# A triangular inverse's first level in a decoder layer: two split steps each become one run of small matmuls, and the first starts later

## The chip, the cores and the metric

The kernel runs on one core of one Trainium2 chip. The metric is device time in microseconds (us) for one execution. TensorE does the matmuls; VectorE (DVE in the profile), ScalarE (ACT) and GpSimd (POOL) move and combine their results; SyncE (SP) and GpSimd issue the DMAs. Matmul results land in PSUM, of which a tile here takes one bank of 128 x 512 float32.

## The reference: one hybrid decoder layer

For 256 tokens of width 1024 the layer computes, cut to what matters:

```python
h = rms_norm(x, norm1_g)
proj = h @ w_in                                  # 5408 columns: RWKV, attention, gates
y_a = rwkv7_time_mix(shift-mixed proj[:1824])    # 8 heads of 64, delta-rule state update per token
y_b = moba_attention(q, k, v)                    # 8 heads; 256 tokens are one block: causal softmax
x = x + (sigmoid(g_a) * (y_a @ w_branch_a) + sigmoid(g_b) * (y_b @ w_branch_b)) @ w_out
h2 = rms_norm(x, norm2_g)
x = x + (gelu(causal_conv3(h2 @ w_up_a)) * (h2 @ w_up_b)) @ w_down
```

and the RWKV recurrence, token by token, with a state of 64 x 64 for each head:

```python
sa = state @ a_t
state = state * w_t + outer(sa, b_t) + outer(v_t, k_t)
y_t = state @ r_t
```

## The kernel before

The recurrence is worked in four chunks of 64 tokens. Within a chunk each of the 8 heads needs the inverse of a unit lower triangular 64 x 64 matrix: 32 inverses (8 heads x 4 chunks), in tiles with an index `u` of 16 and a half `q` of 2. The inverse is built from its diagonal blocks. Blocks of 16 x 16 are inverted on VectorE (`Xb`) and carried by DMAs through DRAM into `X0` and `X`, which hold them where TensorE wants them (lines 757 to 778; DMAs alternate between the queues of GpSimd and SyncE). Then two levels of matmuls follow:

- first level, 16 to 32, for the two 32-halves `h` of each matrix. First step (line 851, tile `pp`): `G` times `X0`, 32 small products for each `h`, copied to `P` by ScalarE (line 857) and VectorE (858). Second step (865, `px`): `X` times `P` for `h = 0`, added into `X0` on VectorE. Third step (880, tile `pxt`): `P` times `X`, 32 small products for each `h`, copied into `X` by ScalarE (888);
- second level, 32 to 64: `pp` again with 32 columns (894), copies to `P`, `pxt` with 32 columns (905), copies into `X`.

A small product here has a 32-row, 16- or 32-column stationary part on a quarter of TensorE's rows; as float32 it is two matmul instructions.

After the inverse the recurrence over the four chunks `c` begins: `pz` (961), `Z0` (965), `pu` (970), `VU` (974, 975), `pS` (981), `Sn` (987 to 990), `pyt` (997, 1002). A third thread, `group_norm`, takes each chunk's output and turns it (`pc`, line 940). Attention turns q and k (`pqk`, 1080), makes scores (`ps`, 1101), a softmax on VectorE and ScalarE (1112 to 1119), turns the weights (`ppt`, 1129) and sums the values (`po`, 1141).

The large products are the weight matmuls. Float32 weights come in chunks of 128 x 1024 (`raw`), are split into a high part (`whi`, ScalarE, 263) and a low part (`wlo`, VectorE, 273), and each product is done three times (high-high, high-low, low-high). In `wst` (lines 301, 303, 306) a block of 12 products of 256 columns stands between two yields; in `xst` (322, 323, 326) a block of 6 products of 512 columns.

The order in which instructions are written is set by hand with generators: `chain` (all of the recurrence), `bulk` (the input projections, the gates, the first branch projection), and, begun by these, `attention` and `group_norm`. Each `yield cost, delay` says how long the piece just written keeps a model clock, and how long after that the thread may go on. The loop takes the first thread in the list that may go on:

```python
cost, lat = next(th[1])
now_t += cost
th[2] = now_t + lat
```

`chain` stands ahead of `bulk` in the list. So a `yield 0, 5.5` in `chain` lets `bulk` write large products for 5.5 units of that clock; a block costs 1.32 (`wst`) or 1.3 (`xst`). With `yield 0.6, 2.5` between two steps two blocks come between. The framework then schedules the instructions of each engine by this order as priority; `tc.high_priority()` moves the marked ones ahead. After the loop the second branch projection (`branch(0, ...)`), the output projection and the channel mixing follow, large products nearly throughout.

Of the kernel before, what the change touches and what calls it, by code (L numbers as in the profile page):

```python
# [36 lines left out]
def body(tc, x, positions, norm1_g, w_in, rwkv_mu, w_decay_up, decay_bias, w_aaa_up,  # L37
# [5 lines left out]
    with ctx:  # L43
# [22 lines left out]
        def b2(name, shape, dt=F32):  # L66
            return sb.tile(shape, dt, name=name, tag="b2", bufs=9)
# [495 lines left out]
        def chain():  # L563
# [275 lines left out]
            def quad(side, h):  # L839
                return slice(64 * side + 32 * h, 64 * side + 32 * h + 32)  # L840

            def two_banks(nm, n):
                return [chp(nm)[:, 0:8 * n].rearrange("p (u n) -> p u n", n=n) for _ in range(2)]

            yield 0, 5.5
            pp = two_banks("pp", 16)
            for h in range(2):
                for i in range(8):
                    for q, a in QA:
                        u = 8 * a + i  # L850
                        pe.matmul(pp[q][quad(1 - a, h), i], G[q][quad(1 - q, h), u, 32 * h:32 * h + 32],
                                  X0[quad(1 - q, h), u, 0:16], start=True, stop=True)
                if h == 0:
                    yield 0.6, 2.5
            P = b2("P", [128, 2, 8, 16])
            with tc.high_priority():
                act.copy(P[:, 0], pp[0])
# [18 lines left out]
            for h in range(2):  # L876
                for u in range(16):
                    for a in range(2):
                        s_ = quad(1 - a, h)
                        pe.matmul(pt[s_.start:s_.start + 16, u], P[s_, u // 8, u % 8],  # L880
                                  X[s_, u, 32 * h + 16:32 * h + 32], start=True, stop=True)
                if h == 0:
                    yield 0.6, 2.5
            for h in range(2):
                for a in range(2):
                    r0 = quad(a, h).start
# [339 lines left out]

        now_t = 0.0
        threads = [["chain", chain(), 0.0], ["bulk", bulk(), 0.0]]
        while threads:
            th = next((h for h in threads if h[2] <= now_t), None)  # L1230
# [191 lines left out]
```

## Time and profile before

| | us |
|---|---|
| median of 3 runs | 407.1 |
| lowest, highest | 406.77, 407.61 |
| the profiled execution, own time | 407.71 |
| its span | 405.6 |
| TensorE busy in the span | 399.1 |
| VectorE, ScalarE, GpSimd busy | 317.8, 234.3, 44.5 |
| first step (L851), first and last matmul start | 103.0, 107.2 |
| third step (L880), first and last matmul start | 114.3, 119.3 |

The profile is one execution; its rows name an engine, a line, an operation, and the tiles it writes and reads (`out<-in`). PE is TensorE's matmuls, PEld its loads of stationary operands. Consecutive matmuls overlap, so a row's busy time says less than the distance between two starts.

### The profile page before, as it was taken

How to read it: one execution, taken by the hardware profiler on the slowest of the kernel's cores; microseconds unless marked ns; L12 is line 12 of the kernel's file. 1: busy time of each engine (PE TensorE's matmuls, PEld its weight loads, DVE VectorE, ACT ScalarE, POOL GpSimd, SP SyncE). 2: the span in 40 equal slices, each digit the busy share in tenths (PEclk: the TensorE clock that was granted, in tenths of full speed). 3: DMA queues.
4: the chain of work that ended last, by engine and by line, in shares of the span. 5: the costliest groups of instructions: out<-in, count | busy, mean ns of one | idle time of the engine just before them, and what ended most of it. 6: DMA issues, size and time to landing. Idle time of an engine off the chain costs nothing.

```text
span 405.6 us, 8306 instructions
## 1 busy us (share of the span) xinstructions
PE 399.1 (98%) x3286; PEld 348.0 (86%) x3286; DVE 317.8 (78%) x539; ACT 234.3 (58%) x395; POOL 44.5 (11%) x72
## 2 busy tenths in 40 slices
PE   6999999999999999999999999999999999999996
PEld 3899899888899898999888888888888888888885
DVE  3888999869576797687965897967869778697694
ACT  5999665365464975453554764555545455365450
POOL 7810510122320010000000000000000000000000
PEclk9999999999999999999999999999999999999999
DMA  8983556755845244446665657566655656656612
GB/s 238 315 255 101 160 155 161 205 137 136 229 114 152 55 156 125 159 136 198 178 197 155 200 161 214 160 210 200 207 185 176 207 178 188 205 174 197 199 56 105
DMA packets 60193, 70.35 MB, mean 173 GB/s; under 512 B 7608, under 2 KB 50506, under 8 KB 60154
## 3 DMA queue, kind: packets, MB, share of 16 engines
q1 hardware_dynamic: 59222, 69.40, 57.2%
q0 software_dynamic: 880, 0.41, 0.6%
q8 instruction: 26, 0.43, 0.4%
q14 instruction: 13, 0.11, 0.1%
q10 hardware_dynamic: 52, 0.01, 0.0%
HBM read 68.37 MB, written 1.44 MB: 172 GB/s over the span
## 4 chain that ended last, share of the span: by engine, by line
PE 92%; DVE 3%; DMA 1%; ACT 1%; issue 1%; POOL 0%; SPq 0%; ACTq 0%
PE acc L1303 20%; PE acc L1308 10%; PE acc L301 8%; PE acc L306 7%; PE acc L303 7%; PE acc L322 5%; PE acc L326 5%; PE acc L323 5%; PE f L1325 4%; PE f L1323 4%; PE f L1327 4%; PE idle L466 1%; DMA x<-in_x_dram 1%; PE pgr L687 1%; DVE sc L1119 1%
## 5 line engine op out<-in xcount | busy, mean ns | idle before, releaser
L263 ACT CAST whi<-raw 128x1024 fp32r<-128x1024 f32 x122 | 127.8, 1052 | 110.8 <-PE acc L1303 42.5
L273 DVE TENSOR_TENSOR wlo<-raw,whi 128x1024 fp32r<-128x1024 f32 x122 | 149.5, 1228 | 38.6 <-PE acc L1308 14.0
L1303 PE MATMUL acc<-hx,whi 128*128 128x512 f32 x352 | 89.5, 396 | 0.0
L1303 PEld LDWEIGHTS acc<-hx,whi 128*128 128x128 f32 x352 | 63.5, 188 | 12.4
L301 PE MATMUL acc<-hx,whi 128*128 128x256 f32 x224 | 56.9, 289 | 0.0
L303 PE MATMUL acc<-hx,whi 128*128 128x256 f32 x224 | 54.6, 279 | 0.0
L1308 PEld LDWEIGHTS acc<-hx,wlo 128*128 128x128 f32 x352 | 46.8, 188 | 4.0
L1308 PE MATMUL acc<-hx,wlo 128*128 128x256 f32 x352 | 47.4, 277 | 0.0
L301 PEld LDWEIGHTS acc<-hx,whi 128*128 128x128 f32 x224 | 42.2, 189 | 2.5 <-issue 1.4
L303 PEld LDWEIGHTS acc<-hx,whi 128*128 128x128 f32 x224 | 42.2, 189 | 0.1
L306 PE MATMUL acc<-hx,wlo 128*128 128x256 f32 x224 | 35.0, 278 | 0.0
L1325 PE MATMUL f<-whi,hb 128*128 128x512 f32 x80 | 31.2, 390 | 0.0
L1323 PE MATMUL f<-whi,hb 128*128 128x512 f32 x80 | 31.2, 390 | 0.0
L1327 PE MATMUL f<-wlo,hb 128*128 128x512 f32 x80 | 31.2, 390 | 0.0
L306 PEld LDWEIGHTS acc<-hx,wlo 128*128 128x128 f32 x224 | 30.0, 189 | 0.0
L1313 DVE TENSOR_REDUCE an<-acc 128x256 f32<-128x512 f32 x22 | 14.2, 685 | 9.4 <-PE acc L1308 9.3
L322 PE MATMUL acc<-whi,hx 128*128 128x512 f32 x48 | 19.5, 406 | 0.0
L323 PE MATMUL acc<-whi,hx 128*128 128x512 f32 x48 | 18.8, 392 | 0.0
L1327 PEld LDWEIGHTS f<-wlo,hb 128*128 128x128 f32 x80 | 15.0, 188 | 3.2
L1323 PEld LDWEIGHTS f<-whi,hb 128*128 128x128 f32 x80 | 15.0, 188 | 2.8
L1325 PEld LDWEIGHTS f<-whi,hb 128*128 128x128 f32 x80 | 15.0, 188 | 2.7
L326 PE MATMUL acc<-wlo,hx 128*128 128x512 f32 x48 | 14.9, 393 | 0.0
(336 smaller groups left out, 627.8 us busy)
## 6 DMA issues: line engine op xcount, KB each, us to landing
raw<-in_w_ffn_up_dram SPq DMA_DIRECT2D x44, 512.0 KB, 4.2
raw<-in_w_in_dram SPq DMA_DIRECT2D x41, 512.0 KB, 3.8
raw<-in_w_ffn_down_dram SPq DMA_DIRECT2D x22, 512.0 KB, 3.9
raw<-in_w_out_dram SPq DMA_DIRECT2D x8, 512.0 KB, 4.0
x<-in_x_dram SPq DMA_DIRECT2D x8, 256.0 KB, 3.7
raw<-in_w_branch_b_dram SPq DMA_DIRECT2D x4, 512.0 KB, 4.1
raw<-in_w_branch_a_dram SPq DMA_DIRECT2D x4, 512.0 KB, 4.3
out_dram<-o SPq DMA_DIRECT2D x3, 256.0 KB
```

The source lines that it names most:

```text
L263: act.copy(hi[:, :k * c], raw[:, :k * c])
L273: eng.tensor_tensor(lo[:, :n], raw[:, :n], hi[:, :n].bitcast(F32), op=OP.subtract)
L301: pe.matmul(om, wh[:, k, ms], xh[:, k0 + k], start=k0 + k + m == 0, stop=False, skip_group_check=True)
L303: pe.matmul(om, wh[:, k, ms], xl[:, k0 + k], start=False, stop=False, skip_group_check=True)
L306: pe.matmul(om, wl[:, k, ms], xh[:, k0 + k], start=False, stop=k0 + k == nk - 1 and m == n - 1, skip_group_check=True)
L322: pe.matmul(ps_[t], xh[:, K, ts], wh[:, k], start=K == 0, stop=False)
L323: pe.matmul(ps_[t], xl[:, K, ts], wh[:, k], start=False, stop=False)
L1303: pe.matmul(ps_[m], wh[:, k, m * 128:m * 128 + 128], hx[:, k0 + k].rearrange("p a s -> p (a s)"), start=k0 + k == 0, stop=False, skip_grou ...
L1308: pe.matmul(ps_[m][:, 0:S], wl[:, k, m * 128:m * 128 + 128], hh[:, k0 + k], start=False, stop=k0 + k == 7, skip_group_check=True)
L1323: pe.matmul(fin[f], hb[:, 0, i, ts], wh[:, 0, cs], start=st, stop=False, skip_group_check=f == 3)
L1325: pe.matmul(fin[f], hb[:, 1, i, ts], wh[:, 0, cs], start=False, stop=False, skip_group_check=f == 3)
L1327: pe.matmul(fin[f], hb[:, 0, i, ts], wl[:, 0, cs], start=False, stop=False, skip_group_check=f == 3)
```

## The change

The delay ahead of the first step goes from 5.5 to 8.0, and the yields between the halves `h = 0` and `h = 1` of the first and of the third step go. Each of these steps is then written as one run of 64 small products, and the first is written after two more blocks of large ones.

```diff
-            yield 0, 5.5
+            yield 0, 8.0
             pp = two_banks("pp", 16)
             for h in range(2):
                 for i in range(8):
...
                         pe.matmul(pp[q][quad(1 - a, h), i], G[q][quad(1 - q, h), u, 32 * h:32 * h + 32],
                                   X0[quad(1 - q, h), u, 0:16], start=True, stop=True)
-                if h == 0:
-                    yield 0.6, 2.5
             P = b2("P", [128, 2, 8, 16])
...
                         pe.matmul(pt[s_.start:s_.start + 16, u], P[s_, u // 8, u % 8],
                                   X[s_, u, 32 * h + 16:32 * h + 32], start=True, stop=True)
-                if h == 0:
-                    yield 0.6, 2.5
             for h in range(2):
```

## The prediction, made before the changed kernel was run

> **What bounds the kernel now.** I read the page's busy shares and its chain, then stretches of the time around the change, then TensorE's waits, then TensorE's instructions in order of time.
>
> ```profile
> span 405.6 us, 8306 instructions
> PE 399.1 (98%) x3286; PEld 348.0 (86%) x3286; DVE 317.8 (78%) x539; ACT 234.3 (58%) x395; POOL 44.5 (11%) x72
> PE 92%; DVE 3%; DMA 1%; ACT 1%; issue 1%; POOL 0%; SPq 0%; ACTq 0%
> ```
>
> TensorE is busy for 98% of the span and 92% of the chain that ended last. The profiled execution took 407.71 us: 405.6 of span and 2.1 around it; it is 0.6 above the median of 407.1 shown.
>
> ```profile
> core 0: us, PE busy (x) PEld busy (x) DVE busy (x) ACT busy (x) POOL busy (x), PEclk, DMA share, GB/s
> 100.00:131.00 31.00, 31.00 (x643) 28.41 (x642) 19.94 (x35) 17.50 (x27) 7.71 (x10) 1.00 0.64 167
> 131.00:178.00 47.00, 46.87 (x610) 42.70 (x609) 36.32 (x81) 31.10 (x82) 4.93 (x4) 1.00 0.41 126
> engine line waited for: us in total, times, longest us
> PEld ppt L1129 <- ACT pT L1130: 0.3, 1, 0.3
> PEld pu L970 <- DVE Z L965: 0.2, 1, 0.2
> ```
>
> The first rows are stretches: the inverse (100 to 131 us) and what follows it to the end of the chain thread (131 to 178). TensorE has no hole in the first and 0.13 us in the second, at the full granted clock. The last rows are TensorE's waits from 84 to 225 us; on another engine's result it waits 0.3 and 0.2 us. So a step of the chain that comes earlier or later gains nothing by itself: large products fill whatever time it leaves. What can change is how long TensorE needs for the same work, and whether it must wait somewhere new. That is read from its order of time:
>
> ```profile
> 101.06 0.62 PE L326 MATMUL acc<-wlo,hx 128*128 128x512 f32 x2
> 101.53 0.39 PE L322 MATMUL acc<-whi,hx 128*128 128x512 f32 x1
> 101.75 0.39 PE L323 MATMUL acc<-whi,hx 128*128 128x512 f32 x1
> ...
> 102.44 0.63 PE L326 MATMUL acc<-wlo,hx 128*128 128x512 f32 x2
> 102.99 0.73 PE L851 MATMUL pp<-X,G 32*32 32x16 f32 x64
> 103.65 0.50 PE L322 MATMUL acc<-whi,hx 128*128 128x512 f32 x1
> 103.99 0.40 PE L323 MATMUL acc<-whi,hx 128*128 128x512 f32 x1
> ...
> 106.61 0.73 PE L851 MATMUL pp<-X,G 32*32 32x16 f32 x64
> 107.27 0.39 PE L301 MATMUL acc<-hx,whi 128*128 128x256 f32 x1
> ...
> 110.29 0.73 PE L865 MATMUL px<-P,X 32*32 32x16 f32 x64
> ...
> 114.28 0.97 PE L880 MATMUL pxt<-X,P 32*16 32x16 f32 x64
> 115.18 0.66 PE L1080 MATMUL pqk<-ident,qkv 128*128 128x128 f32 x4
> ...
> 118.50 0.97 PE L880 MATMUL pxt<-X,P 32*16 32x16 f32 x64
> 119.40 0.66 PE L1080 MATMUL pqk<-ident,qkv 128*128 128x128 f32 x4
> ```
> ```profile
> L851 PE MATMUL pp<-X,G x128: 177/178/199, 103.0 to 107.2; 32*32 32x16 f32 x128
> L880 PE MATMUL pxt<-X,P x128: 170/172/186, 114.3 to 119.3; 32*16 32x16 f32 x128
> ```
>
> Each row has start, length, line, tiles and count; the last two give shortest, median and longest single matmul in ns. A small float32 product is two matmuls, so "x64" is 32 products. Between two runs of small ones lie two blocks of 12 or 6 large products, with four transposes (L1080) at some.
>
> **What a run costs.** Undisturbed, from the start of the last two products of a block (L326, 101.06) to the second product of the next block (101.75) takes 0.69 us. With a run of 64 matmuls between, 102.44 to 103.99 takes 1.55. The run costs 0.86. Within it, the row's 0.73 less the last matmul's own 0.178 is 63 steps: 0.0088 us each, 0.56 for 64. The other 0.30 is fixed: entering from large products and getting back to their rhythm. L880's steps are (0.97 - 0.172)/63 = 0.0127 us. All of this lies on the path, since TensorE is never idle.
>
> **The change, part by part.** The scheduler's own times (cost, delay) only order the program; I follow them through the code. Nothing is added to or removed from any engine's work, no DMA is issued elsewhere in its queue, no wait is added.
>
> (1) First step later. With a delay of 8.0 for 5.5, two more blocks, 12 products of 512 columns, go first; the step starts when 102.44 + 2 x (102.44 - 101.06) + 0.55 = 105.75. It is then one run of 128 matmuls; 0.66 for the first half as now (103.65 - 102.99) and 0.56 for 64 more steps bring the large products back at 106.97, against 107.27. The blocks ahead of it cost nothing, since they had to be done; had there been none, the wait would be 2.76 us. Behind the step on TensorE stand the next block and, two blocks on, L865. Its readers are two copies:
>
> ```profile
> L857 ACT COPY P<-pp x1: 258/258/258, 109.2 to 109.2; 128x128 f32<-128x128 f32 x1
> L771 POOL DMA_DIRECT2D X<-d x4: 562/564/583, 99.7 to 101.4; - x4
> DMA to landing us min/median/max: 2.0/2.1/2.1
> ```
>
> The ScalarE copy ends at 109.46 and L865 starts at 110.29; if that copy stays and L865 comes 0.3 earlier, 0.5 is left. The rows of the DMAs say that the blocks of X0 for h = 1 land by 101.4 + 2.1 = 103.5: the later run has all its inputs and can't stall there. Saved: one fixed cost, 0.30.
>
> (2) Third step in one run. The second half follows the first at once, not after two blocks and a transposed group. 64 products take 128 x 0.0127 = 1.63 us, and one fixed cost goes: 0.30. Bounds: the trace has runs of 64 of these matmuls and none of 128. If their steps stay as quick, each part saves 0.30. If all of the long run of part 1 went at the slower row's step, it would take 128 x 0.0039 = 0.50 more and lose 0.20; if only its second half did, 0.25 more, and 0.05 would be left. I take 0.30, by the row of the same matmul. Sum so far -0.60, ends -0.60 and -0.10, with -0.35 between.
>
> The Trainium skill, "TensorE: Matmul & The Clock Gate", section "Part 3: Packing small matmuls", has a packed run last one matmul plus about 4 ns for each further one. By it a merge would save just one matmul, here 0.178 and 0.172, and the sum of (1) and (2) would be -0.35. The trace differs: 8.8 and 12.7 ns a step, and 0.30 of fixed cost around a run.
>
> (3) The rest of the chain moves one slot (two blocks and a transposed group, 118.50 - 114.28 = 4.2 us) forward against large products and attention. Following the yields, separate groups of small products from the first step to the end of the chain are 19 before: pp, pp, px+pqk, pt+pqk, pt+pqk, pp32+pqk, pxt32+scores, pu0+scores, pS0+scores, pz1, pu1, pS1+turn, pz2+pc0, weighted+turn+pu2, pS2+turn+pc1, pz3, weighted+pu3, pS3+pc2, pc3. The trace has this order up to 128 us. After: pp, px+pqk, pt+pqk, pp32+pqk, pxt32+pqk, pu0+scores, pS0+scores, pz1, pu1+scores, pS1, pz2+pc0, turn+pu2, pS2+weighted+turn+pc1+pz3, pu3+turn, pS3+pc2+weighted, pc3: 16. Two of the three lost are (1) and (2). The third comes from other neighbours; inside a group a change of shape also costs, so its worth lies between 0 and 0.30. I take 0.10, nearer to 0, because its members are of differing shapes.
>
> The Trainium skill, "TensorEngine Tiling (Array Packing)", section "Key Properties", says that a change of tiling mode drains TensorE. By it joined groups of different shape save little: from pxt32 on I count 35 changes of mode before and 34 after; at half of 0.30 for one that makes (3) -0.15, where a whole group less would make it -0.30. No run yet shows which holds.
>
> (4) Pace of large products:
>
> ```profile
> 175.29 0.62 PE L306 MATMUL acc<-ybh,wlo 128*128 128x256 f32 x4
> 176.65 0.62 PE L306 MATMUL acc<-ybh,wlo 128*128 128x256 f32 x4
> 179.94 0.64 PE L306 MATMUL acc<-ybh,wlo 128*128 128x256 f32 x4
> 181.35 0.63 PE L306 MATMUL acc<-ybh,wlo 128*128 128x256 f32 x4
> ```
>
> The same block of 12 takes 1.36 us before the last small group (177.3) and 1.41 after it. The rhythm seems set on re-entry and kept. After pc3 there are 5 blocks of the first branch projection and 8 of the second now, and 7 + 8 in the new order. If the re-entry sets the slow pace again, two more blocks run slow: +0.10. If the fast one, 15 x 0.05 = -0.75, less what these are counted slow now (13 x 0.05): a gain of 0.65.
>
> (5) Waits. At pu0 and after, two blocks still lie between a chain step and the next in nearly all places. The two waits quoted (0.3 and 0.2) may go, or as many come: 0, between -0.5 and +0.5.
>
> Sum: -0.30 - 0.30 - 0.10 + 0.10 + 0 = -0.60 us. The profiled execution would become 407.1, the median 406.5.
>
> **The rivals.**
>
> The fast pace: pc3's re-entry leaves the fast rhythm. For it: the blocks just before 177 run at 1.36. Against: pc3's own transposes stay, and after them it was slow. -0.60 - 0.10 - 0.65 = -1.35: 405.75 as median.
>
> The saving is smaller, or a step doesn't gain: the longer run of small matmuls loses what the re-entry saved (-0.35 by (2)), or one wait of half a microsecond comes. For it: no run of 128 is in the trace. (The packing rule of the Trainium skill's page "TensorE: Matmul & The Clock Gate", above, comes out here too.) -0.1 to -0.35: about 406.9.
>
> The other side: VectorE late in the recurrence.
>
> ```profile
> L273 DVE TENSOR_TENSOR wlo<-raw,whi 128x1024 fp32r<-128x1024 f32 x122 | 149.5, 1228 | 38.6 <-PE acc L1308 14.0
> 127.86 1.16 PE L1101 MATMUL ps<-qkT,qkT 64*128 64x128 f32 x16
> ```
>
> In the new order the first softmax is written right behind pS0, not ahead of it, so its long VectorE operations fall together with Sn, which pz1 waits for. Between pS0 and pz1 TensorE has scores (1.1) and one block (1.4): 2.5 us. Two operations of the size of L273 (1.23) ahead of Sn just exhaust that; three make TensorE wait 1.2 to 1.4 us and a second such place (Z before pu1, which waits 0.2 already) decides: -0.60 + 1.4 + 0.7 = +1.5, 408.6. Against: in that stretch VectorE is busy for 36.32 of 47 us and so has 10.7 left, and Sn is marked high priority.
>
> That the change doesn't do what it says: the framework may order TensorE's instructions otherwise than they are written; then the halves would stay apart and the time 407.1. I hold it unlikely; it is counted with the smaller saving.
>
> **How the numbers follow.** This measurement can tell about 0.2% (0.8 us) from no change. Likeliest case, -0.60 with -0.2 to -1.1 as its own range: 0.49, of which 0.17 lies beyond -0.8. Fast pace: 0.24. Smaller saving: 0.14. VectorE late: 0.13, nearly all above +0.8. So faster 0.41, same 0.47, slower 0.12. The range runs from 405.3, below the fast pace by half the wait term, to 407.7, where a wait of one long VectorE operation has used up the saving (-0.60 + 1.23).
>
> **What would show it.** L851 as one row of 128 matmuls starting near 105.7, L880 as one of 128 near 114; large products resuming 0.3 us earlier behind the first and another 0.3 behind the second; L905 some 3.7 us earlier. TensorE's idle in 131 to 178 stays near 0.1. The blocks after the last L940 show 1.41 (my forecast) or 1.36. Wrong if steps within a run of 128 are slower than 8.8 and 12.7 ns, if TensorE waits for Sn or Z, or if products outside these stretches change their pace.

## The result, and the profile after

| | before | after |
|---|---|---|
| median, us (8 runs each) | 407.4 | 409.6 |
| lowest to highest | 406.3 to 408.3 | 408.6 to 412.0 |
| ratio, 95% interval | 1 | 1.006 (1.0034 to 1.0086) |
| profiled execution, its span | 407.71, 405.6 | 410.01, 408.1 |

The changed kernel is 2.2 us slower. I had forecast 0.6 faster. In half of after's eight runs, the profiled one among them, the granted clock lies a little below full speed (0.992 to 0.996) and the median is 410.5, against 408.8 in the other four; what that adds is kept apart below.

Rows of after's page, then its stretches of time (the columns are those of the stretches before):

```profile
span 408.1 us, 8311 instructions
PE 400.1 (98%) x3286; PEld 348.7 (85%) x3286; DVE 318.2 (78%) x539; ACT 235.2 (58%) x395; POOL 44.0 (11%) x72
q8 instruction: 26, 0.43, 0.4%
```
```profile
core 0: us, PE busy (x) PEld busy (x) DVE busy (x) ACT busy (x) POOL busy (x), PEclk, DMA share, GB/s
100.00:120.00 20.00, 17.82 (x406) 16.20 (x405) 12.62 (x25) 9.69 (x17) 7.06 (x9) 0.91 0.59 148
112.50:116.00 3.50, 3.50 (x19) 3.50 (x18) 3.29 (x12) 0.69 (x1) 0.44 (x1) 0.51 0.60 154
131.00:178.00 47.00, 46.06 (x596) 41.79 (x597) 37.96 (x82) 30.53 (x82) 4.03 (x4) 1.00 0.41 125
```

Two things are new. Between 100 and 120 us, where TensorE had no hole before, 2.18 us are idle, and from 112.5 to 116 the granted clock is half. And between 131 and 178 the idle time is 0.94 us, against 0.13.

After's order of time on TensorE shows the first at once:

```profile
104.98 1.26 PE L851 MATMUL pp<-X,G 32*32 32x16 f32 x128
106.17 0.39 PE L301 MATMUL acc<-hx,whi 128*128 128x256 f32 x1
...
109.12 0.25 PE L863 MATMUL px<-P,X 32*32 32x16 f32 x8
111.56 0.65 PE L863 MATMUL px<-P,X 32*32 32x16 f32 x56 [2.18 <-issue]
112.14 0.77 PE L1076 MATMUL pqk<-ident,qkv 128*128 128x128 f32 x4
112.56 0.56 PE L301 MATMUL acc<-hx,whi 128*128 128x256 f32 x1
112.92 0.41 PE L303 MATMUL acc<-hx,whi 128*128 128x256 f32 x1
113.13 0.41 PE L301 MATMUL acc<-hx,whi 128*128 128x256 f32 x1
...
117.06 1.69 PE L878 MATMUL pxt<-X,P 32*16 32x16 f32 x128
118.68 0.66 PE L1076 MATMUL pqk<-ident,qkv 128*128 128x128 f32 x4
```

Both steps did become one run (x128). But the second step, `px`, stops after 8 of its 64 matmuls (four products), stands from its last start at 109.19 to 111.56, and goes on by itself. "issue" is the profile's word for an engine that waited for nothing that it shows. The matmuls where it stops carry no wait on a semaphore; only the first two of the run do, and those had begun. So it isn't data. Large products then start every 0.21 us (112.92 to 113.13) for three microseconds, where 0.113 is usual.

TensorE's waits in after, first those at its weight loads, then those in the recurrence that fall on another engine:

```profile
engine line waited for: us in total, times, longest us
PEld px L863 <- issue: 2.3, 1, 2.3
PEld pz L957 <- issue: 1.0, 3, 0.5
PEld pu L966 <- issue: 0.7, 2, 0.6
```
```profile
PE pu L966 <- DVE Z L961: 0.4, 1, 0.4
PE pz L957 <- DVE mx L1109: 0.4, 1, 0.4
```

**Where the time went.** Stage by stage in the profiled executions, from start to start of matmuls (us). The end of `px` is the start of its last matmul, the output projection begins with its first transpose, and "without hole" is experiment e3 below:

| stage | before | after | without hole |
|---|---|---|---|
| first large product (L301) to `pp` | 84.89 | 87.64 | 87.64 |
| `pp` to the end of `px` | 7.85 | 7.04 | 4.68 |
| `px` to the first `pu` | 21.05 | 18.45 | 16.84 |
| first `pu` to the last `pc` | 45.58 | 47.53 | 47.54 |
| last `pc` to the output projection | 29.37 | 31.43 | 31.42 |
| sum | 188.74 | 192.09 | 188.12 |

From before to after the sum grows by 3.35. The second row holds the hole (7.04 - 4.68 = 2.36) and the third the half clock (18.45 - 16.84 = 1.61). Without these the change would gain 0.62, close to the 0.60 forecast; how much of that is luck is said below. The rest of the span differs by the start (the first large product came 0.76 us earlier in after's execution) and 0.05 at the end: 3.35 - 0.81 = 2.54, the difference of the spans to 0.04.

**What TensorE waited for.** The page lists a DMA queue that carries instructions: q8, 26 packets of 16 KB. There are 2 x 3286 matmuls and loads in the profile, so one packet holds about 253 of them: TensorE's own program comes in blocks through the same DMA engines as the weights. Here are the stretches of 0.1 us in which the block in question begins, in before (104.2 to 104.3 us) and in after (108.85 to 108.95), each behind the stretch ahead of it (103 to 104.2; 105 to 108.85):

```profile
DMA packets 786, 0.08 MB, mean 67 GB/s; under 512 B 749, under 2 KB 786, under 8 KB 786
...
q8 instruction: 1, 0.02, 74.9%
```
```profile
DMA packets 1320, 1.28 MB, mean 334 GB/s; under 512 B 66, under 2 KB 1320, under 8 KB 1320
...
q8 instruction: 1, 0.02, 70.0%
```

In before the block begins at 104.26, ahead of the burst of raw weights, and is there by 105.5. In after it begins at 108.89, behind 3.9 us in which weights moved at 334 GB/s, takes 1.12, and TensorE goes on at 111.56. From the packet's end (110.01) to the end of the hole are 1.55 us more, and in the five other kernels below that have a hole 1.2 to 1.5. The profile doesn't show what fills them, but the even distance ties each hole to its packet.

Two things come together. The request, which no row shows, must come later, by where the program now stands: a run of 128 small matmuls and their loads is 256 instructions, a whole block, in 1.2 us. And the weights stand where they stood: the first of the burst is issued 85.1 us behind the first large product, in before 85.0. So the request must now fall behind them.

The Trainium skill, "Runtime: NRT & Kernel Launch", section "Instruction fetch mechanics", has each engine's program refilled in blocks of 16 KiB, 256 instructions, by the sequencer's own DMA queue, and calls the cost of a crossing mostly hidden. The trace agrees on the block (16 KB, about 253 profiled instructions) and not on the cover: 2.36 us are open here.

### The profile page after: what moved, and what is told of

The parts are those of the page before. It is cut to its first block, busy times and chain, and to the rows that moved or that the text cites. A ratio compares the mean times of both kernels' runs of the same rounds, so it can differ in the third digit from the quotient of the medians.

```text
span 408.1 us, 8311 instructions
## 1 busy us (share of the span) xinstructions
PE 400.1 (98%) x3286; PEld 348.7 (85%) x3286; DVE 318.2 (78%) x539; ACT 235.2 (58%) x395; POOL 44.0 (11%) x72
## 4 chain that ended last, share of the span: by engine, by line
PE 90%; DVE 4%; issue 2%; DMA 1%; POOL 1%; ACT 1%; SPq 0%; ACTq 0%; POOLq 0%
PE acc L1299 20%; PE acc L1304 10%; PE acc L301 8%; PE acc L303 7%; PE acc L306 7%; PE acc L322 5%; PE acc L326 4%; PE acc L323 4%; PE f L1321 4%; PE f L1323 4%; PE f L1319 4%; DVE wlo L273 1%; PE idle L466 1%; DMA raw<-in_w_in_dram 1%; PE pgr L687 1%
## 5 line engine op out<-in xcount | busy, mean ns | idle before, releaser
L1299 PEld LDWEIGHTS acc<-hx,whi 128*128 128x128 f32 x352 | 63.4, 188 | 12.4
L301 PE MATMUL acc<-hx,whi 128*128 128x256 f32 x224 | 57.6, 291 | 0.0
L303 PE MATMUL acc<-hx,whi 128*128 128x256 f32 x224 | 55.3, 282 | 0.0
L301 PEld LDWEIGHTS acc<-hx,whi 128*128 128x128 f32 x224 | 43.0, 192 | 2.6 <-issue 1.5
L303 PEld LDWEIGHTS acc<-hx,whi 128*128 128x128 f32 x224 | 43.0, 192 | 0.1
```

The costliest lines, as they stand in the source:

```text
L301: pe.matmul(om, wh[:, k, ms], xh[:, k0 + k], start=k0 + k + m == 0, stop=False, skip_group_check=True)
L303: pe.matmul(om, wh[:, k, ms], xl[:, k0 + k], start=False, stop=False, skip_group_check=True)
L1299: pe.matmul(ps_[m], wh[:, k, m * 128:m * 128 + 128], hx[:, k0 + k].rearrange("p a s -> p (a s)"), start=k0 + k == 0, stop=False, skip_grou ...
```

## The experiments

The first four ask which part brings the loss, and of what kind it is. Theory S is the supply of instructions, V is VectorE late in the recurrence; stages are those of the table.

**e1, the first step alone** (after, with the third step's yield put back):

```diff
+                if h == 0:
+                    yield 0.6, 2.5      # third step
```


> Only the first step is changed (delay 8.0, one run); the third step keeps its two halves. The hole of 2.3 us in the px run lies ahead of the third step. Theory S (TensorE's next block of instructions was asked for inside the later first step, while the DMA engines were full of weight loads, and came late): the instructions up to px are those of the changed kernel, so the hole of 2 to 2.5 us at px is there again, and the time is 408.0 to 409.5 us. Theory R (the regrouped tail behind the merged third step is the loss): no loss here, 406.5 to 407.

Measured 409.55, ratio 1.0068 (1.0048 to 1.0087). The loss is here in full, and the hole at the same place:

```profile
109.72 0.25 PE L863 MATMUL px<-P,X 32*32 32x16 f32 x8
112.25 0.65 PE L863 MATMUL px<-P,X 32*32 32x16 f32 x56 [2.28 <-issue]
112.83 0.66 PE L1078 MATMUL pqk<-ident,qkv 128*128 128x128 f32 x4
113.25 0.37 PE L301 MATMUL acc<-hx,whi 128*128 128x256 f32 x1
113.45 0.28 PE L303 MATMUL acc<-hx,whi 128*128 128x256 f32 x1
```

Here the large products went on at full pace behind a hole as long. So the half clock is a second cost that the hole brings on in some executions. The later stages (45.61 and 29.41) are before's: the third step isn't part of this loss.

**e2, the third step alone** (before without that step's yield):

```diff
-                if h == 0:
-                    yield 0.6, 2.5      # third step
```


> Only the third step is changed; the first keeps its early start and its two halves. Theory S: the block is asked for at 103.3 us, before the weight loads fill the DMA engines, as in the kernel before; no hole at px; one run's fixed cost saved: 406.4 to 407.2 us. Theory R (tail): 408 us or more, with TensorE waiting for VectorE's Sn and Z.

Measured 407.2, ratio 0.9995 (0.998 to 1.001). No hole, and 188.74 in sum: nothing gained. The `px` stage of this run holds a wait of 0.2 for `X0` in the first step; `px` to `pu` falls by 4.20, `pu` to `pc` grows by 1.96 and the last stage by 2.05. The waits at `pz` and `pu` (1.0 and 0.7) are here too, so they don't need the first step's change. e10 below has them with the third step split, so they come with a chain that stands one slot earlier, whichever merge brings that.

**e3, the burst taken away** (after, with three chunks of `w_in` not loaded but set to zero, so that part of the input projection is left out):

```diff
-                for ks in ...: nc.sync.dma_start(rv[:, ks], ap[:, ks])
+                popped[0] += 1
+                if popped[0] in (32, 33, 34):
+                    pool.memset(raw, 0.0)
+                else:
+                    for ks in ...: nc.sync.dma_start(rv[:, ks], ap[:, ks])
```


> The changed kernel, with three weight chunks (those whose loads are issued at 102.4 to 103.7 us) set to zero by GpSimd in place of being loaded, so that part of w_in is left out. Theory S: the instruction block starts within about 1 us of being asked for, not 3.7; the hole at px goes or shrinks below 0.5 us; 406 to 407 us. Theory B (a run of 128 small matmuls with their weight loads uses up its instructions faster than any fetch delivers): the hole stays at 2 us or more, 408 to 409.5. Theory D (px waits for data, X's DMAs or the copy P): unchanged by the weight loads or a little better, hole over 1 us.

Measured 406.77, ratio 0.9994 (0.9984 to 1.0005). TensorE has after's matmuls in after's order, and the hole is gone:

```profile
105.34 1.26 PE L856 MATMUL pp<-X,G 32*32 32x16 f32 x128
106.53 0.39 PE L306 MATMUL acc<-hx,whi 128*128 128x256 f32 x1
...
109.47 0.72 PE L868 MATMUL px<-P,X 32*32 32x16 f32 x64
110.13 0.55 PE L1081 MATMUL pqk<-ident,qkv 128*128 128x128 f32 x3
```

The block begins at 106.57, 1.2 us after `pp` starts, where after took 3.9. It is the transfers, not the order on TensorE, that made it late.

**e4, the program shifted** (43 tiny matmuls in place of three of the eight warming ones at the start, some 80 more instructions):

```diff
-            keep_warm(8)
+            keep_warm(5)
+            for i in range(43):
+                g = slice(32 * (i % 4), 32 * (i % 4) + 32)
+                pe.matmul(p[g, 0:16], ones[g, 0:32], ones[g, 0:16], start=True, stop=True)
```


> The changed kernel with 80 more TensorE instructions at the very start (43 tiny matmuls in place of 3 of the large ones that only keep TensorE warm while it waits for x). Nothing else moves; only the place of the 256-instruction block borders shifts by 80. Theory S: the border that fell some 37 instructions into the first step falls behind its instruction 200, the one ahead of it some 40 instructions before the step's blocks are over: the block asked for late is needed only behind px, near 113 us, and the hole goes. 405.8 to 407 us. Theory D (data wait): the hole stays where it is, 408 to 410 us. Theory B: a hole of 2 us somewhere else.

Measured 407.75, ratio 1.0013 (1.0002 to 1.0025). The border between blocks now comes ahead of `pp`, its block begins at 101.07, before the burst, and `px` has no hole; the sum is 188.37. But with fewer warm matmuls at the start the first transposes are slower (two groups of eight take 1.97 and 1.91 us, in before 1.10 and 1.09), and the first large product comes at 19.23, in before at 18.10 and in after at 17.34. That hides the gain. e5 mends it.

**e5, shifted and warm** (after, with `keep_warm(8)` kept and 40 tiny matmuls behind it):

> The shift of 80 instructions again, now by 40 tiny matmuls on top of the large warming ones, so that TensorE's clock is as warm at the start as in the other kernels (with fewer warming ones the first transposes ran at half speed and the start cost 1.2 to 1.9 us). Theory S (late instruction block): no hole at px, as in the run before, and the start of the kernel before: 406.3 to 407.0 us, from the first large product to the output projection's first transpose 188.1 to 188.5 us (before 188.7, changed 192.1). If the shift's gain had been something else: 408 or more.

Measured 406.92, ratio 0.9998 (0.9984 to 1.0013). All loads are as in after, the block begins at 100.11, and the hole is gone:

```profile
105.43 1.26 PE L854 MATMUL pp<-X,G 32*32 32x16 f32 x128
...
109.56 0.73 PE L866 MATMUL px<-P,X 32*32 32x16 f32 x64
```

The sum is 188.11, 0.63 less than before's. Together with e3 this settles the cause: the same hole goes by taking away the transfers or by asking for the block earlier, with nothing else in the change touched.

**e6 and e12, the hole brought into before** (before with 80, and with 92, of the tiny matmuls behind `keep_warm(8)`):

> The kernel before, nothing of the change, with 160 more TensorE instructions at the start (80 tiny matmuls). Theory S: a block border now falls at the second half of the first step (106.6 us), in the middle of the weight loads; its block starts only when these end (about 109 to 111 us) and TensorE, which needs it near the end of the px run at 110.8, stands 1 to 2.8 us: 408 to 410 us. Theory that the later or longer first step itself is at fault: no hole, 407.2 plus at most 0.5.

> The kernel before with a shift of 184 instructions, the second try to give it a hole: in the shift of 160 the block was asked for at 108.1 us and came just in time, because X0's DMAs were 1.1 us late. Theory S: the border now lies some 10 instructions into the second half of the first step; the block, asked for at 105 to 106.6 us, starts behind the weight loads at 109 to 109.5 and is there at about 112; it is needed some 90 instructions into px, near 110.7: a hole of 1 to 1.5 us without a semaphore in px; 408 to 409 us. Theory that only the long run of the changed kernel can run dry: none, 407.2.

Measured 407.75, ratio 1.0012 (1.0000 to 1.0024), and 407.33, 0.9994 (0.9984 to 1.0003). Neither shows such a hole. What e6 shows at the first step is a wait for data, which e12 has with 0.4:

```profile
PE pp L854 <- DMA X<-d: 1.1, 2, 0.9
```

These two are misses. In e6 the block begins at 109.41, in e12 at 106.33, and in both TensorE had not yet run out. The profile shows no request, only where a packet begins, and the delay between them varies (see e9), so I could not place a border to the microsecond.

**e9, a smaller shift** (after with 15 tiny matmuls):

> The changed kernel with only 30 more TensorE instructions at the start (15 tiny matmuls). Theory S counts blocks of about 255 instructions: the late block is still asked for inside the first step (37 instructions in, not 67), so it comes as late, about 111.5 us, but it is needed 30 instructions sooner, some 19 large products behind the first step, near 108.4 us: the hole moves from the px run into the large products ahead of it and grows from 2.4 to about 3 us; 408.5 to 411 us. Theory that a shift of instructions as such removes the hole, or that px waits for data: no hole, 407, or the hole at px as before.

Measured 407.86, ratio 1.0002 (0.9987 to 1.0017). The hole moved where the count puts it, out of `px` and into the large products ahead of it:

```profile
108.18 0.28 PE L303 MATMUL acc<-hx,whi 128*128 128x256 f32 x1
108.69 0.28 PE L301 MATMUL acc<-hx,whi 128*128 128x256 f32 x1 [0.23 <-issue]
...
109.49 0.72 PE L866 MATMUL px<-P,X 32*32 32x16 f32 x64
```

Counted along TensorE's matmuls, loads and semaphore instructions in the trace, the instruction behind the hole is number 1985 in after, in e1 and here, though here it is a large product with other inputs. No wait on data can do that; a border of a block does. Its size was a miss: 0.51 from start to start, since the block began at 106.15. That is 1.26 us behind `pp`, nearly as soon as in e3, though weights moved at 352 GB/s from 104.9 to 106.1 (its request lies 30 instructions earlier in the program than after's). So a burst can hold a block back and need not. e2 and e7 have the same program up to there, and their blocks began 1.6 and 3.6 us behind `pp` (103.85 and 106.01); e7 has no hole all the same, as it reaches number 1985 only at 109.66. What decides the delay these runs don't show.

**e8 and e11, the old tail** (after with 40, and with 50, tiny matmuls, and a pause behind the third step, so that the steps after it stand where they stood before):

```diff
+            yield 0.01, 2.5      # behind the third step
```


> Both steps in one run each, the first late, the shift of 80 instructions, and behind the third step a second yield (0.01, 2.5), which gives attention its place in an empty slot: from there on the written order of all threads is that of the kernel before. Theory S + V: no hole, no new waits in the recurrence, two fixed costs of 0.3 saved: from the first large product to the output projection's first transpose 188.1 us (before 188.74) if the large products behind the last pc go at 118 ns, 187.5 at 113; 406.0 to 406.7 us. If merging saves nothing by itself: 188.7 and 407.2.

> Both steps in one run, the first late, attention kept in its old place behind the third step (yield 0.01, 2.5), and a shift of 100 instructions in place of 80. With 80 a second, smaller hole (0.7 us) stood behind the third step, where a block was used up 0.7 us before the next had come. Theory S: with 100 each of the three blocks between 104 and 120 us comes 0.9 us or more ahead of its use: no hole, 187.9 us from the first large product to the output projection's first transpose at the slow pace (before 188.74), 406.1 to 406.6 us. If it is no matter of block borders, the 0.7 us stay.

Measured 406.85, ratio 1.0004 (0.9983 to 1.0024), and 407.97, 1.0032 (1.0010 to 1.0054). The recurrence is quick again: 45.60 in both, and in e8 TensorE is idle for 0.14 us there, so the new waits come from where the merge puts the recurrence:

```profile
131.00:178.00 47.00, 46.86 (x610) 42.68 (x609) 36.32 (x81) 31.10 (x82) 4.93 (x4) 1.00 0.40 124
```

But a second hole opens behind the run of the third step in e8 and inside it in e11 (rows of e8, then of e11):

```profile
115.39 0.66 PE L1080 MATMUL pqk<-ident,qkv 128*128 128x128 f32 x4
116.47 0.28 PE L301 MATMUL acc<-hx,whi 128*128 128x256 f32 x1 [0.43 <-issue]
```
```profile
113.65 1.64 PE L881 MATMUL pxt<-X,P 32*16 32x16 f32 x122
116.20 0.25 PE L881 MATMUL pxt<-X,P 32*16 32x16 f32 x6 [0.91 <-issue]
```

The instruction behind it is number 2497 in both and 2496 in e4 (a gap of 0.25 there): 512 on from 1985, two blocks. e11 was meant to move this hole away, and only moved it from behind the run into it, and made it longer: 1.09 us from start to start, in e8 0.70.

**e7, less work for VectorE** (e2, with the softmax's last multiplication done for 8 keys only, so most of its normalization is left out):

```diff
-                dve.tensor_tensor(sc, sc, sm[:, :, None].to_broadcast([128, nh, nk]), op=OP.mult)
+                dve.tensor_tensor(sc[:, :, 0:8], sc[:, :, 0:8], sm[:, :, None].to_broadcast([128, nh, 8]), op=OP.mult)
```


> The version with the third step alone in one run (no hole; TensorE waits some 1.3 us for pz, pu and pc in the recurrence), with the softmax's last multiplication left out for all but 8 keys of each head (three VectorE operations of about 1.2 us become 0.1 to 0.3). Theory V (these waits are VectorE's: Sn and Z stand behind long softmax operations): the waits for pz and pu fall from 1.7 to under 0.7 us and the stretch from pu0 to the last pc from 47.5 to about 46.6; 406.3 us. Theory O (the waits come from the order of TensorE's own steps, from semaphores or from PSUM): unchanged.

Measured 406.58, ratio 0.9987 (0.9978 to 0.9996). `pu` to `pc` is 46.98, against 47.54 in e2, and the wait at `pz` falls from 1.0 to 0.5. At `pu` the wait on `Z` stays (0.5, in e2 0.4). So this one multiplication is 0.56 us of the longer stage. What else holds `pu` I have not separated.

**e10, the first step merged but not moved** (delay 5.5, third step split):

> Only the yield inside the first step is taken out; it starts at its old time (102.3 to 103.0 us). Theory S: the block is asked for before the weight loads fill the DMA engines, no hole without a semaphore. Instead the second half now stands where it may have to wait for X0's last DMAs (land about 103.5) and px comes two blocks after, near 107, ahead of ScalarE's copy of P at 109.2: a wait of 0.5 to 2.5 us with a semaphore; 406.6 to 408.5 us.

Measured 407.86, ratio 1.0010 (0.9995 to 1.0025). There is no hole from the supply, but `px` now waits 0.4 on VectorE:

```profile
PE px L863 <- DVE r L1028: 0.4, 1, 0.4
```

Whether that is an operation of attention in the way of `P`'s copy, as the row's `r` suggests, was not tried. The later start avoids this wait: after has none at `px` but the hole. Without the delay the first step's merge alone brings the chain a slot forward, and the waits at `pz` and `pu` (1.0 and 0.7) are here as in e2; `pu` to the last `pc` takes 47.72.

No version that does the whole work (e3 and e7 leave some out) beats before by what can be measured.

## Why the prediction was wrong

**Step (1), the late first step, failed.** It said that the run "has all its inputs and can't stall there", and that no wait is added. The run itself was right: `pp` starts 0.77 before the forecast 105.75, as the whole execution stood earlier, and the large products are back 1.19 us behind its start (104.98 to 106.17), where 0.66 + 0.56 = 1.22 was forecast; its steps are (1.26 - 0.178)/127 = 8.5 ns, against 8.8 in the split step. What I left out of "inputs" is TensorE's own program: its next block came late, and TensorE stood 2.36 us for it in `px`, where the sum had no wait. Without the hole, from the first large product to the end of `px` takes 92.32 in e3 for 92.74 before: 0.42 saved, where the term said 0.30.

I asked of each transfer what data it delays. The page's list of queues has a row for instructions, which the prediction did not use, and the trace of before already had the block begin at 104.26, 1.2 us behind the issue of the burst's first weights (103.10). That the step was moved toward that burst, and made to use up a block in one go, could have been read from it.

**The half clock** was in no rival. The rows at 112.92 and 113.13 and the granted 0.51 carry it; e1 shows that a hole of this length need not bring it. A granted clock below 0.997 came in 4 of after's 8 executions, 1 of 4 of e1, 1 of 11 of e5, 2 of 12 of e8 and 5 of 12 of e11, and in none of the 99 of before that ran beside the experiments. The one of e5 took 409.68 and may have had a hole; the profiled one has none. The Trainium skill, "TensorE: Matmul & The Clock Gate", section "Part 1: The HAM clock gate", has the clock halved after an idle window of about 3.4 us, and says that the windows run freely, without regard to where work starts. The trace doesn't bear out the length: no 3.4 us were idle, and 2.36 us here halved the clock where 2.46 in e1 did not. So the length of the hole alone doesn't decide; windows that run freely would fit that, but no run here shows where they lie.

**Step (2), the third step.** It ran as one, 118.68 - 117.06 = 1.62 for the forecast 1.63. Its gain is seen in e8 and e11, where all behind it keeps its old order: with the same products, `px` to the first `pu` takes 21.32 and 21.84, in before 21.05. The second hole costs 0.59 of it in e8 (1.97 from the last transpose ahead of it to the twelfth product behind, in e3 1.37) and 1.10 in e11 (its run takes 2.62 from first to last start, in e3 1.52). Without it 20.7 is left in both: 0.3 saved, as forecast. In e2 the sum doesn't change at all, as TensorE's idle time of 0.88 from 131 to 178 us and the 0.2 for `X0` use up this gain and that of the pace.

**Step (3), regrouping**, at 0.10, isn't borne out. Without the hole, 0.42 by step (1), 0.3 by step (2) and 0.76 by the pace (below) would be 1.48, and 0.62 was saved. So the regrouped part lost some 0.86, about what TensorE's idle time grew by (0.81), and by this estimate nothing is left for a group saved.

**Step (4), the pace, went the other way.** I took the slow rhythm (+0.10) and made the fast one a rival (-0.65). These are the products (shortest, median and longest in ns) from 174 to 186 us, of before and of after:

```profile
L306 PE MATMUL acc<-ybh,wlo x32: 276/281/284, 173.9 to 184.5; 128*128 128x256 f32 x32
```
```profile
L306 PE MATMUL acc<-ybh,wlo x26: 276/276/277, 177.4 to 186.0; 128*128 128x256 f32 x26
```

Before's turn slow within the stretch, after's stay fast, and so do those of e2, e3 and e5, the versions with the new order. From start to start the medians behind the last `pc` are 118 and 113 ns. The last stage grew by 2.06 for two more blocks, where two slow ones (1.41 each) would be 2.82: 0.76 less than step (4) had for the stage, where the rival had 0.75. But the written order alone doesn't set the pace. e6 has before's order, and its products there are fast: 114 ns from start to start, where before, e1, e8, e11 and e12 have 118, and 28.72 for the last stage, where before takes 29.37 for the same products:

```profile
L306 PE MATMUL acc<-ybh,wlo x32: 276/276/284, 175.2 to 185.6; 128*128 128x256 f32 x32
```

**Step (5), waits at 0, failed in size**: TensorE's idle time in 131 to 178 grew by 0.81, beyond the 0.5 that I gave as its end. The two rows with `Z` and `mx` name the places of the rival "VectorE late", `pu` and `pz`. That rival had the mechanism and the places, but not the price: 0.4 at `pu` where it had 0.7, and 0.4 at `pz` where it had 1.4.

So terms of opposite sign, fast pace against new waits, nearly cancel, and 0.62 without the hole comes out beside the forecast 0.60 partly by chance. The wrong sign comes from the hole and its clock alone: 2.36 + 1.61 in the profiled execution. Against the medians, -0.62 + 2.36 leaves +1.7 for executions at full clock, and +1.5 was measured for them (408.84 less 407.36). The others lie 1.6 above these, as much as the half clock's 1.61, and the median of all eight, +2.2, lies between.

## What to carry to other kernels

Joining small matmuls into long runs uses up TensorE's program faster: 128 small matmuls with their loads are one block of it in 1.2 us. Look at the queue of instructions in the profile, find where its packets begin against bursts of weight loads, and keep a run of small instructions away from a burst or the burst away from it. A hole inside a run whose instructions carry no wait, and which stays at the same instruction count when the program is shifted, points to supply, not data.

## What the runs showed of the hardware

That a block of instructions can be held back by weight transfers: it began 1.2 us after `pp` without the burst (e3) and 3.9 with it (after), though 1.26 within a burst in e9. That a late block stops TensorE: in the six kernels with such a hole TensorE went on 2.2 to 2.9 us after the block's packet began. That the hole is up to 2.46 us, at instruction 1985 in three kernels and 2496 or 2497 in three others. That the rhythm of large products, 113 or 118 ns from start to start, holds for the next 30 us and is worth 0.65 us here for the same products in the same order (e6 against before); what sets it stays open.
